# RMSNorm with repeated rows: ScalarE's table load moved ahead of gamma, and gamma issued in six pieces instead of seven

## The chip, the cores and the metric

The kernel runs on one core of one Trainium2 chip. The metric is the device time of one execution in microseconds. Executions of one kernel differ by some tenths of a microsecond, so every comparison below, unless it says otherwise, is between runs of the same rounds on the same chip.

## The reference

```python
x: (8, 512, 2048) float32, gamma: (2048,) float32
x_rep  = np.repeat(x, 2, axis=1)                       # every row twice
rms    = np.sqrt((x_rep ** 2).mean(axis=-1, keepdims=True) + 1e-6)
return (x_rep / rms * gamma[None, None, :])            # (8, 1024, 2048)
```

Each of the 4,096 rows is normalised once and written twice: 33.56 MB are read, 67.11 MB are written.

## The kernel before

The rows come in eight tiles of 128 partitions x 4 rows. A tile's buffer holds eight rows per partition; the load fills the last four, the scaled rows go to the even places and are copied to the odd ones, and one store of 8.39 MB takes all eight. There are three buffers, so three loads can go ahead of the first store, and the fourth needs the first store done.

```python
def load(i, eng, parts=1):                 # the first tile comes in two halves
    y = rows.tile([P, K * R, D], f32, name="y")
    step = K // parts
    for k in range(0, K, step):
        at = K * (R - 1) + k
        eng.dma_start(out=y[:, at : at + step, :], in_=x_t[i, :, k : k + step, :])
# ... cut: store (SyncE), square (ScalarE: Square with row sum, then Sqrt),
# ... scale (VectorE: reciprocal, then y * rstd * gamma), repeat (a copy)

def compute(i):
    for k in range(K):
        scale(i, k, square(i, k))
    repeat(i, 0, K // 2, nc.scalar.copy)
    repeat(i, K // 2, K, nc.vector.tensor_copy)

load(0, nc.sync, parts=2)
gamma_b = singles.tile([P, D], f32, name="gamma_b")
cuts = [0, *range(D // 4, D + 1, D // 8)]              # 512, then 6 x 256 values
for c0, c1 in zip(cuts, cuts[1:]):
    nc.scalar.dma_start(out=gamma_b[0:1, c0:c1], in_=gamma[c0:c1].partition_broadcast(1))
nc.gpsimd.partition_broadcast(out_ap=gamma_b[:], in_ap=gamma_b[0:1, :])
# ... cut: eps_t
load(1, nc.sync)
load(2, nc.sync)
loads_after = {2: (3, 4, 5), 4: (6, 7)}
for i in range(ntiles):
    compute(i)
    store(i, 0, K)
    for j in loads_after.get(i, ()):
        load(j, nc.sync)
```

The source names no semaphore. They are given to the transfers when the program is built: eight serve all loads, stores and gamma pieces, and a transfer that gets one again is held, in its issuing queue, until the transfer that had it has landed.

## Time and profile before

| | kernel before |
|---|---|
| median of 3 runs | 239.9 us (239.46 to 239.91) |
| profiled span | 237.9 us |
| gamma whole (the broadcast's wait ends) | 12.4 us |
| first scaling on VectorE | 14.92 us |
| first store issued | 27.05 us |
| first store landed | 52.8 us |

The times of single events are read from the timeline, the last one from the chain of waits. The lines themselves, and how to read them, stand in the prediction below.

### The profile page before, as it was taken

How to read it: one execution, taken by the hardware profiler on the slowest of the kernel's cores; microseconds unless marked ns; L12 is line 12 of the kernel's file. 1: busy time of each engine (PE TensorE's matmuls, PEld its weight loads, DVE VectorE, ACT ScalarE, POOL GpSimd, SP SyncE). 2: the span in 40 equal slices, each digit the busy share in tenths (PEclk: the TensorE clock that was granted, in tenths of full speed). 3: DMA queues.
4: the chain of work that ended last, by engine and by line, in shares of the span. 5: the costliest groups of instructions: out<-in, count | busy, mean ns of one | idle time of the engine just before them, and what ended most of it. 6: DMA issues, size and time to landing. Idle time of an engine off the chain costs nothing.

```text
span 237.9 us, 287 instructions
## 1 busy us (share of the span) xinstructions
DVE 96.5 (41%) x73; ACT 101.0 (42%) x106; POOL 2.5 (1%) x5
## 2 busy tenths in 40 slices
DVE  0049999960000000059999960000199990000000
ACT  2697999900000000099999920000599960000000
POOL 0030000000000000000000000000000000000000
DMA  7999998989899998999998999989998989999994
GB/s 265 436 446 441 441 441 353 530 353 496 386 452 430 397 485 353 441 441 441 441 518 364 464 419 430 452 369 430 435 518 364 518 364 485 397 452 430 408 474 176
DMA packets 2464, 100.69 MB, mean 423 GB/s; under 512 B 279, under 2 KB 285, under 8 KB 286
## 3 DMA queue, kind: packets, MB, share of 16 engines
q1 hardware_dynamic: 2448, 100.66, 98.5%
q14 instruction: 2, 0.02, 0.0%
q10 hardware_dynamic: 14, 0.01, 0.0%
HBM read 33.56 MB, written 67.11 MB: 423 GB/s over the span
## 4 chain that ended last, share of the span: by engine, by line
DMA 58%; ACT 12%; DVE 9%; issue 1%; POOLq 1%; ACTq 1%; SPq 0%
DMA y<-in_x_dram 33%; DMA out_dram<-y 21%; ACT sq L64 8%; DVE y L74 7%; DMA gamma_b<-in_gamma_dram 4%; ACT y L81 3%; DVE y L81 2%; ACT rms L68 1%; POOLq L136 1%; ACTq L95 1%; DVE rstd L73 0%; POOLq L96 0%; SPq L56 0%
## 5 line engine op out<-in xcount | busy, mean ns | idle before, releaser
L64 ACT ACTIVATE sq<-y 128x2048 f32<-128x2048 f32 x32 | 59.7, 1865 | 87.8 <-DMA y<-in_x_dram 87.8
L74 DVE SCALAR_TENSOR_TENSOR y<-y,rstd,gamma_b 128x2048 f32<-128x2048 f32 x32 | 75.3, 2352 | 4.1 <-POOL gamma_b L96 3.0
L73 DVE RECIPROCAL rstd<-rms 128x1 f32<-128x1 f32 x32 | 5.0, 158 | 94.6 <-ACT rms L68 94.3
L81 ACT COPY y<-y 128x4096 f32<-128x4096 f32 x8 | 28.7, 3590 | 1.4 <-DVE y L74 1.4
L81 DVE COPY y<-y 128x4096 f32<-128x4096 f32 x8 | 18.3, 2294 | 0.3
L68 ACT ACTIVATE rms<-ss,eps_t 128x1 f32<-128x1 f32 x32 | 9.4, 295 | 1.0
L64 ACT ACTIVATION_READ_ACCUMULATOR sq<-y 128x1 f32 x32 | 6.0, 187 | 0.0
L64 ACT ACT_TABLE_LOAD x1 | 1.3, 1283 | 3.0 <-issue 3.0
L96 POOL PARTITION_BROADCAST gamma_b<-gamma_b x1 | 2.3, 2294 | 12.2 <-DMA y<-in_x_dram 12.2
L68 ACT ACT_TABLE_LOAD x1 | 1.3, 1283 | 0.0
L98 DVE MEMSET eps_t<- 128x1 f32 x1 | 0.1, 59 | 0.8 <-PEq L125 0.8
L125 POOL MEMSET const-uint8-127<- 128x1 uint8 x1 | 0.1, 102 | 0.0
L125 POOL MEMSET const-bfloat16-1.0<- 128x1 bf16 x1 | 0.1, 101 | 0.0
L125 POOL MEMSET const-float32-0.0<- 128x1 f32 x1 | 0.1, 98 | 0.2 <-issue 0.2
L125 POOL MEMSET const-float32-1.0<- 128x1 f32 x1 | 0.1, 98 | 0.0
## 6 DMA issues: line engine op xcount, KB each, us to landing
y<-in_x_dram SPq DMA_DIRECT2D x7, 4096.0 KB, 14.6
y<-in_x_dram SPq DMA_DIRECT2D x2, 2048.0 KB, 7.4
out_dram<-y SPq DMA_DIRECT2D x8, 24.4
gamma_b<-in_gamma_dram ACTq DMA_DIRECT2D x6, 1.0 KB
gamma_b<-in_gamma_dram ACTq DMA_DIRECT2D x1, 2.0 KB
```

The costliest lines, as they stand in the source:

```text
L64: nc.scalar.activation(out=sq[:], in_=ys[i][:, K * (R - 1) + k, :], func=Act.Square, accum_out=ss[:])
L68: nc.scalar.activation(out=rms[:], in_=ss[:], func=Act.Sqrt, scale=inv_d, bias=eps_t[:])
L73: nc.vector.reciprocal(out=rstd[:], in_=rms[:])
L74: nc.vector.scalar_tensor_tensor(out=ys[i][:, R * k, :], in0=ys[i][:, K * (R - 1) + k, :], scalar=rstd[:], in1=gamma_b[:], op0=Alu.mult, o ...
L81: copy(out=y_r[:, k0:k1, 1, :], in_=y_r[:, k0:k1, 0, :])
L95: nc.scalar.dma_start(out=gamma_b[0:1, c0:c1], in_=gamma[c0:c1].partition_broadcast(1))
L96: nc.gpsimd.partition_broadcast(out_ap=gamma_b[:], in_ap=gamma_b[0:1, :])
L98: nc.vector.memset(eps_t, eps)
L125: nc = _bacc.Bacc("TRN2", target_bir_lowering=False, num_devices=1)
L136: with _tile.TileContext(nc) as tc:
```

## The change

It means to give ScalarE one table load in place of two and take it out of the first tile's work; and to take one transfer out of the start, so that the eight semaphores suffice and the first tile's second half need not wait for a gamma piece.

```diff
     load(0, nc.sync, parts=2)
+
+    nc.scalar.preload_act_table(Act.Sqrt)
     gamma_b = singles.tile([P, D], f32, name="gamma_b")
-    cuts = [0, *range(D // 4, D + 1, D // 8)]
+    cuts = [0, D // 4, *range(D // 2, D + 1, D // 8)]
```

## The prediction

> **What bounds the kernel now.** I read the page's transfer rows first, since the kernel reads 33.56 MB and writes 67.11 MB with little arithmetic.
>
> ```profile
> DVE 96.5 (41%) x73; ACT 101.0 (42%) x106; POOL 2.5 (1%) x5
> ...
> DMA packets 2464, 100.69 MB, mean 423 GB/s; under 512 B 279, under 2 KB 285, under 8 KB 286
> ...
> q1 hardware_dynamic: 2448, 100.66, 98.5%
> ```
>
> No compute engine works even half of the 237.9 us span, while the one queue that carries all loads and stores occupies its sixteen engines for 98.5% of it. To see where the other 1.5% lies I cut the span into stretches (columns: stretch, length, busy us of the three engines with counts, clock, share of the DMA engines, GB/s; packets count where they start, so a short stretch can pass 1.00):
>
> ```profile
> 0.00:2.00 2.00, 0.06 (x1) 0.00 (x0) 0.19 (x4) 1.00 0.45 91
> 2.00:4.00 2.00, 0.00 (x0) 1.02 (x1) 0.00 (x0) 1.00 0.77 295
> 4.00:8.00 4.00, 0.00 (x0) 0.26 (x1) 0.00 (x0) 1.00 0.97 414
> 8.00:12.00 4.00, 0.17 (x1) 3.85 (x5) 0.00 (x0) 1.00 1.02 439
> 12.00:16.00 4.00, 1.08 (x1) 3.94 (x6) 2.29 (x1) 1.00 1.07 463
> 16.00:27.00 11.00, 10.86 (x9) 9.56 (x9) 0.00 (x0) 1.00 1.02 441
> 27.00:33.00 6.00, 5.89 (x6) 5.90 (x10) 0.00 (x0) 1.00 1.19 448
> ...
> 60.00:120.00 60.00, 16.09 (x13) 18.63 (x21) 0.00 (x0) 1.00 1.01 435
> 120.00:180.00 60.00, 28.32 (x23) 28.77 (x32) 0.00 (x0) 1.00 0.98 425
> 180.00:232.00 52.00, 16.00 (x11) 14.08 (x14) 0.00 (x0) 1.00 1.01 440
> ```
>
> The DMA is full from 4 us to 232 us. Nothing drops where the computing starts (16 us), nor where the first store joins (27 to 33 us). So I treat the kernel as **transfers at full rate, plus an edge at each end**. From 33 us to 232 us the rows (with 430 GB/s in the 27 us not printed) average 432.6 GB/s; 100.69 MB at that rate is 232.8 us. In the first 4 us only 2 x 91 + 2 x 295 = 772 KB move instead of 1,730 KB: 2.2 us lost. 232.8 + 2.2 = 235.0; the other 2.9 us of the span are the last packets, the last landing and the closing barrier. The timed median, 239.9 us, is 2.0 us over the profiled span, which no change here touches.
>
> **A trap in the chain of waits.** In order of time it starts with gamma and the first tile's arithmetic:
>
> ```profile
> 2.69 9.71 DMA gamma_b<-in_gamma_dram
> ...
> 12.55 2.35 POOLq L136
> ...
> 14.92 2.35 DVE y L74
> ...
> 27.05 25.77 DMA out_dram<-y
> ```
>
> Read literally, gamma's arrival sets the end: an earlier gamma means an earlier first store. But that store's 25.77 us hold a queue. It is 8.39 MB (4,096 KB of loaded rows, doubled), which at 432.6 GB/s takes 19.4 us; the other 6.4 us it waited behind loads and for its first bytes. The three loads together are 12.58 MB, or 29.1 us at that rate; with the 2.2 us lost at the start they last till about 31.3 us. A first packet follows its issue by about 1 us (issue at 0.72 us, nothing moved before 1 us, 91 GB/s by 2 us). So the store, issued at 27.05 us, could have come till about 30.3 us: **3 us of slack**, an estimate from these rows.
>
> **What the Trainium skill says.** "ScalarE: Activation LUTs", section What ACT_TABLE_LOAD costs: about 1283 ns for a load, the same for every set, plus a drain of about 1380 ns at each switch. The trace has two loads of 1283 ns, so the first number agrees; the drain does not show, as the root begins at 11.43 us, 0.01 us after the load that began at 10.14. The page doesn't say in which sets Square lies; that one load serves Square and Sqrt is the change's claim. "DMA: Bandwidth & Descriptors", section Specifications, gives a fabric ceiling of 435 GB/s and an HBM limit of some 358 per core; the trace keeps 432.6, so here the first is the wall. The same page, section Queues, rings and completion order, says that each DMA engine takes turns between the queue rows that have work. Gamma's seven small pieces landing only by 12.4 us amid full-rate loads fits that.
>
> **The change, part by part.** The start of the timeline:
>
> ```profile
> 0.72 2.23 ACTq L95 DMA_DIRECT2D gamma_b<-in_gamma_dram  x7
> 0.72 8.20 SPq L52 DMA_DIRECT2D y<-in_x_dram  x4
> 2.98 1.28 ACT L64 ACT_TABLE_LOAD   x1 [2.98 <-issue]
> 10.14 1.28 ACT L68 ACT_TABLE_LOAD   x1
> 12.60 2.29 POOL L96 PARTITION_BROADCAST gamma_b<-gamma_b  x1 [12.17 <-DMA y<-in_x_dram]
> 14.92 2.35 DVE L74 SCALAR_TENSOR_TENSOR y<-y,rstd,gamma_b 128x2048 f32<-128x2048 f32 x1 [3.00 <-POOL gamma_b L96]
> ```
>
> *Table loads, two to one.* The first load now (2.98 us) lies in idle time: ScalarE waits for x until 8.12 us. The second is in ScalarE's work; without it the first root starts at about 10.15 instead of 11.43 us, 1.28 us sooner. But the first scaling waits from 11.92 to 14.92 us for the broadcast of gamma, not for the root. On the path: 0.
>
> *The load ahead of gamma.* ScalarE now issues gamma from 0.72 us; with 1.28 us of load first, from about 2.0 us. Cost to gamma: up to +1.28 us.
>
> *Six pieces, not seven.* One issue fewer is 0.27 us. More telling is how the pieces land: seven in 9.71 us after the last issue ended at 2.69. The first landed early, since the second load's 0.9 us wait for it (below) was over at about 2 us; the six others then shared about 8 us amid the packets of x, an estimated 1.2 to 1.3 us each. Afterwards all six pieces come into the busy period, and six did so before as well: the early one is the one saved. So gamma is whole at 12.4 us if the DMA engines set the pace, or at most 1.3 us later; I take +0.6. The broadcast, four scalings and a copy from gamma to the store took 27.05 - 12.42 = 14.63 us and stay, so the store is issued at 27.7 us (27.0 to 28.4), inside the slack. Cost at the end: 0.
>
> *The wait of the second half.* The queue's own waits:
>
> ```profile
> SPq L52 <- DMA y<-in_x_dram: 5.7, 1, 5.7
> SPq L52 <- DMA gamma_b<-in_gamma_dram: 0.9, 1, 0.9
> ```
>
> Nothing in the source makes x wait for gamma. Seven pieces and two halves are nine transfers; the eight semaphores that they use in the trace are then one too few, so the second half waited for the first piece. With six pieces there are eight, and the 0.9 us wait goes. It was worth nothing: the first half alone, 2.1 MB, keeps the engines busy for about 5 us, and the stretch from 4 to 8 us, in which one half hands over to the other, shows 0.97. The second tile's load keeps a wait for the eighth transfer before it, till about 8 us as now, with the first tile moving until about 12 us. On the path: 0.
>
> *Sum.* 0 + 0 + 0 + 0, with perhaps 0.1 us either way from who issues first at 0.72 us. Later stages keep their order and sizes.
>
> **Rivals.** *Gamma really is on the path*, as the chain says: then 0.6 to 1.3 us later gamma gives 240.5 to 241.2. The full windows from 16 to 33 us speak against it. *Gamma gets stuck behind the second half*, now issued at about 1.1 us, ahead of every piece: pieces that start only when the first tile has moved, at 12 us, need 6 x 1.26 = 7.6 us, so gamma is whole at about 19.6 us and the store goes at 34.2, some 4 us past the slack: 243.6 us, +1.6%. The taking of turns between queues speaks against it. *The second tile's load waits for the second half* (landing at about 12.5 us) and the DMA runs dry for 1 to 2 us: 241.5 us. Against it: of the eight transfers the first semaphore should go to the first half or to a gamma piece. *The start is the cost* and an earlier second half fills it: at most the 2.2 us of the first 4 us, 237.7 us; but the first half alone has packets enough there.
>
> **Range and chances.** All terms on the path are zero, so I predict the middle of the before-runs, slightly under the median: 239.7 us. The before-runs span 0.45 us; the bad rivals add 1 to 4 us at perhaps one in eight together, gains are at most tenths. Range 239.1 to 240.6. Two per cent is 4.8 us, more than any rival gives: faster 0.01, same 0.98, slower 0.01.
>
> **What would show it.** In the changed kernel's profile: one table load, at about 0.7 us, none before the first root; the second half issued at about 1.1 us with no wait for gamma; the broadcast starting between 12.5 and 14 us; the first store at 27.0 to 28.4 us, landing still at about 52.8 us; the DMA stretches from 4 to 232 us full as now; span 237.5 to 238.5 us. It is wrong if the DMA share dips near 12 us or between 28 and 36 us, or if the first store lands over 1 us later.

## The result, and the profile after

The changed kernel takes **239.67 us** (median of 6 runs, 239.34 to 239.86) against 239.91 us (6 runs, 239.4 to 240.17) of the kernel before. The ratio is 0.9993, with a 95% interval of 0.998 to 1.0007: the same. (The record calls a difference under 2% "the same"; here the interval holds 1 too. A ratio is the mean time of one kernel's fast runs over that of the other's of the same rounds, so it is not quite the ratio of the medians.)

The changed kernel's page shows what of the work has gone: ScalarE has 1.1 us and one instruction less. The queue of loads and stores is as full as it was.

```profile
DVE 96.5 (41%) x73; ACT 99.9 (42%) x105; POOL 2.5 (1%) x5
...
q1 hardware_dynamic: 2448, 100.66, 98.7%
```

The timeline of its start (start us, length us, engine, line, operation; in brackets the idle time before it and what ended that):

```profile
0.72 1.28 ACT L93 ACT_TABLE_LOAD   x1 [0.72 <-PEq L127]
0.72 8.28 SPq L52 DMA_DIRECT2D y<-in_x_dram  x4
0.75 1.93 ACTq L97 DMA_DIRECT2D gamma_b<-in_gamma_dram  x6
10.24 0.29 ACT L68 ACTIVATE rms<-ss,eps_t 128x1 f32<-128x1 f32 x1
11.41 2.29 POOL L98 PARTITION_BROADCAST gamma_b<-gamma_b  x1 [10.98 <-DMA gamma_b<-in_gamma_dram]
13.73 2.35 DVE L74 SCALAR_TENSOR_TENSOR y<-y,rstd,gamma_b 128x2048 f32<-128x2048 f32 x1 [3.01 <-POOL gamma_b L98]
25.86 0.35 SPq L56 DMA_DIRECT2D out_dram<-y  x1
```

Two things are to be seen. Gamma's first piece is issued at 0.75 us, **while** the table load runs from 0.72 to 2.00 us. And everything that hangs on gamma comes 1.19 us earlier than before: the broadcast (12.60 to 11.41 us), the first scaling (14.92 to 13.73 us), the first store (27.05 to 25.86 us).

Its chain of waits shows where those 1.19 us go (start us, us, what):

```profile
2.41 8.80 DMA gamma_b<-in_gamma_dram
...
25.86 26.76 DMA out_dram<-y
52.64 48.38 DMA y<-in_x_dram
```

The store that starts 1.19 us earlier takes 26.76 instead of 25.77 us to land, so that it lands at 52.62 instead of 52.82 us. Nearly all of the gain was spent in the queue behind the loads.

### The profile page after: what moved, and what is told of

Same layout as the page of the kernel before. It is cut to its first block, busy times and chain, and to the rows that moved or that the text cites. A ratio compares the mean times of both kernels' runs of the same rounds, so it can differ in the third digit from the quotient of the medians.

```text
span 237.6 us, 284 instructions
## 1 busy us (share of the span) xinstructions
DVE 96.5 (41%) x73; ACT 99.9 (42%) x105; POOL 2.5 (1%) x5
## 2 busy tenths in 40 slices
DMA packets 2462, 100.69 MB, mean 424 GB/s; under 512 B 278, under 2 KB 282, under 8 KB 284
## 4 chain that ended last, share of the span: by engine, by line
DMA 58%; ACT 12%; DVE 9%; issue 1%; POOLq 1%; ACTq 0%; SPq 0%
DMA y<-in_x_dram 33%; DMA out_dram<-y 21%; ACT sq L64 8%; DVE y L74 7%; DMA gamma_b<-in_gamma_dram 4%; ACT y L81 3%; DVE y L81 2%; ACT rms L68 1%; POOLq L138 1%; ACTq L97 0%; DVE rstd L73 0%; ACT L93 0%; POOLq L98 0%; SPq L56 0%
## 5 line engine op out<-in xcount | busy, mean ns | idle before, releaser
L93 ACT ACT_TABLE_LOAD x1 | 1.3, 1283 | 0.7 <-PEq L127 0.7
```

Source lines behind the costliest of these rows:

```text
L93: nc.scalar.preload_act_table(Act.Sqrt)
```

## The experiments

**The theory.** The time is set by 100.69 MB at the full rate of the sixteen transfer engines. The first store may be issued until the loads ahead of it run out; earlier than that is worth nothing, later counts in full. **The rival** is the chain of waits taken at its word: the first store is on the path, so each microsecond on gamma or the first tile's arithmetic moves the end by one. A second question is why gamma came earlier, where the prediction had it later.

### The first store, made late in steps

Three kernels are the changed one, with the first tile's last VectorE copy done two, four or six times more. The copies write the same data again, so the results stay right.

```diff
         repeat(i, K // 2, K, nc.vector.tensor_copy)
+        for _ in range(4 if i == 0 else 0):            # 2, 4 and 6
+            repeat(i, K // 2, K, nc.vector.tensor_copy)
```

> The changed kernel, with the last VectorE copy of the first tile done twice more (2.29 us each, same data), so that the first store goes 4.6 us later, at about 30.4 us. The loads' last packets start at about 32.4 us and a store's first packet follows its issue by about 1 us, so my theory has 1 us of slack left: 239.7 us, no change. If the first store is on the path, as the chain of waits says, +4.6 us: 244.3 us.

> Four more copies, 9.2 us: the store goes at about 35.0 us, past the slack (31.4 us) by 3.6 us. My theory: the transfer engines run dry near 33 to 36 us and the time is 239.7 + 3.6 = 243.3 us (range 242.5 to 244.5). If the first store is on the path: 248.9 us. If the transfers have spare room later on to make up for it: 239.7 us.

> Six more copies, 13.8 us: the store goes at about 39.6 us, 8.2 us past the slack. My theory: 239.7 + 8.2 = 247.9 us (range 247 to 249), 4.6 us more than with four copies, since past the slack each microsecond counts in full. If the first store is on the path: 253.5 us. If there is room to make up: less than 4.6 us between this run and the one with four copies.

| copies added | first store issued | median | over the kernel before of the same rounds (239.4 us) | ratio, 95% interval |
|---|---|---|---|---|
| 2 | 30.31 us | 240.07 us (4 runs) | 0.67 us | 1.0017 (0.999 to 1.0043) |
| 4 | 34.97 us | 244.74 us (4 runs) | 5.34 us | 1.0217 (1.0195 to 1.024) |
| 6 | 39.74 us | 249.52 us (4 runs) | 10.12 us | 1.0417 (1.0395 to 1.0439) |

The issue times stand in the SyncE timelines, one line of each of the three runs:

```profile
30.31 24.67 SPq L56 DMA_DIRECT2D out_dram<-y  x3
34.97 24.67 SPq L56 DMA_DIRECT2D out_dram<-y  x3
39.74 24.67 SPq L56 DMA_DIRECT2D out_dram<-y  x3
```

From four to six copies the issue moves by 4.77 us and the time by 4.78 us: past the slack each microsecond counts in full. Going back at that slope to the time of the kernel before gives a break-even at 34.97 - 5.34 = 29.63 us, and 39.74 - 10.12 = 29.62 us from the other run. So, with these copies in, the first store may be issued until about **29.6 us**, give or take half a microsecond by the intervals; the run with two copies, 0.7 us past it, is within the noise. By this the kernel before had 29.6 - 27.05 = 2.6 us of slack and the changed kernel has 3.8 us. The rival, which wanted 244.3, 248.9 and 253.5 us, is out.

My own expectations were off, by about 1.4 us with four copies and 1.6 us with six, outside both ranges. A small part is where the transfers run dry. I had taken 32.4 us in the changed kernel for the start of the loads' last packets. The trace shows the loads' completion marks and the first store's packets starting there; the loads' last data packets start by 31.0 us and take 2.0 us each, which fits the first store's packets already sharing the engines with them. Where the store is late they take 1.2 us and the loads are through sooner: with four copies the trace shows no data packet at work between 31.8 and 35.8 us, 4.0 us where I had expected 3.6. The stretches (columns as in the prediction) show the same hole, first of the changed kernel, then with six copies:

```profile
32.00:36.00 4.00, 3.93 (x4) 4.00 (x2) 0.00 (x0) 1.00 1.21 524
36.00:40.00 4.00, 3.96 (x3) 3.94 (x7) 0.00 (x0) 1.00 0.94 410
```

```profile
32.00:36.00 4.00, 3.93 (x3) 0.00 (x0) 0.00 (x0) 1.00 0.00 0
36.00:40.00 4.00, 3.93 (x4) 0.00 (x0) 0.00 (x0) 1.00 0.00 0
```

VectorE is as busy in one as in the other. The DMA columns tell them apart: nothing moves for 8 us.

The larger part of the miss is not lost at the first store at all. The landings, from the completion marks in the traces (us, in brackets the difference from the kernel before):

| | kernel before | 2 copies | 4 copies | 6 copies |
|---|---|---|---|---|
| first store | 52.82 | 51.66 (-1.16) | 55.79 (+2.97) | 60.57 (+7.75) |
| fourth tile's load | 101.15 | 100.55 (-0.60) | 105.23 (+4.08) | 109.99 (+8.84) |
| fourth store | 140.22 | 140.89 (+0.67) | 145.30 (+5.08) | 150.37 (+10.15) |

Between the first and the fourth store each of the three loses another 1.8 to 2.4 us. The copies hold back the later tiles too (the second store is issued at 47.15 us with four copies, at 39.22 us in the kernel before), but what costs these 2 us was not tested. So 29.6 us is a break-even of the whole program with the copies in it. The hole alone says something later: the store's first packet followed its issue by 0.8 us (34.97 to 35.81 us) and the engines ran dry at 31.8 us, so a store issued by about 31.0 us, an estimate from these, leaves no hole.

### The transfers alone

```diff
-        for k in range(K):
-            scale(i, k, square(i, k))
-        repeat(i, 0, K // 2, nc.scalar.copy)
-        repeat(i, K // 2, K, nc.vector.tensor_copy)
+        nc.vector.tensor_copy(out=ys[i][:, 0:K, :], in_=ys[i][:, K : 2 * K, :])
```

> Wrong result on purpose: the arithmetic of each tile is replaced by one VectorE copy of the four loaded rows, so all loads and stores stay as they are and every store can go earlier. If the transfers alone set the time, 239.0 to 240.0 us, though the first store goes at about 18 to 19 us, 7 us or more earlier. If computing at the start or in later stages is on the path, faster by the part that it holds: 7 us for the first store alone (233 us).

Measured: 239.24 us (5 runs), against 239.5 us (9 runs) of the kernel before; ratio 0.999, interval 0.9977 to 1.0002. The result is wrong, as intended. Its SyncE timeline has the first store 9.2 us earlier than in the kernel before:

```profile
17.84 20.36 SPq L56 DMA_DIRECT2D out_dram<-y  x3
```

With all the arithmetic gone but one copy a tile, and every store free to go sooner, at most 0.23% is won, and perhaps nothing. That bounds what any change to the table loads, gamma or the arithmetic could have earned here.

### Gamma in one piece

```diff
-    cuts = [0, D // 4, *range(D // 2, D + 1, D // 8)]
+    cuts = [0, D]
```

> Gamma in one transfer. My theory of the turns: the first piece gets in before the packets of x (landed at about 2.1 us), each later one waits its turn, so one piece is whole by about 2.2 us, the broadcast is over before x has arrived (8.2 us), the first scaling starts at about 10.7 us, the third waits for the second half at about 13 us, and the first store goes at about 24 us, 3 us earlier than before. Time: if the transfers set the end, 239.7 us, within 0.3% of before. If the first store is on the path, as the chain of waits says, 236.9 us (1.3% faster).

Measured: 240.33 us (5 runs) against 239.5 us; ratio 1.0021 (1.0007 to 1.0035). Gamma was whole at 2.93 us, later than the 2.2 us expected; the first scaling came as expected and the first store about 1 us earlier:

```profile
3.02 2.29 POOL L98 PARTITION_BROADCAST gamma_b<-gamma_b  x1 [2.59 <-DMA gamma_b<-in_gamma_dram]
...
10.76 2.35 DVE L74 SCALAR_TENSOR_TENSOR y<-y,rstd,gamma_b 128x2048 f32<-128x2048 f32 x1
```

The broadcast now starts 9.6 us earlier than before and the first store is issued at 22.89 us, 4.16 us earlier. The end does not come earlier. The kernel is 0.2% slower, if anything; I did not pursue a difference of that size, and its cause stays open.

### Which part brought gamma forward, and what the table load does

The first of these kernels has the six pieces but no preloaded table, the second the preload but the seven old pieces.

```diff
-    nc.scalar.preload_act_table(Act.Sqrt)              # six_only: the changed kernel without this
-    cuts = [0, D // 4, *range(D // 2, D + 1, D // 8)]  # preload_only: the changed kernel with
+    cuts = [0, *range(D // 4, D + 1, D // 8)]          #   the old cuts
```

> Six pieces, both table loads where they were. If the dropped piece alone explains gamma's earlier arrival (about 1.2 us a piece), gamma is whole at 11.2 us, the broadcast starts at 11.4 and the first scaling at about 13.7 us, although the root waits for its table load until 11.43 us; first store at 25.9 us; no queue wait for gamma. If the preload had a share in it, the first scaling is later than 13.9 us. Time within 0.3% of before.

Measured: 239.97 us (4 runs) against 239.5 us; ratio 1.0017 (1.0003 to 1.003), within the 0.3% expected.

```profile
11.11 2.29 POOL L96 PARTITION_BROADCAST gamma_b<-gamma_b  x1 [10.69 <-DMA gamma_b<-in_gamma_dram]
...
13.44 2.35 DVE L74 SCALAR_TENSOR_TENSOR y<-y,rstd,gamma_b 128x2048 f32<-128x2048 f32 x1 [1.49 <-POOL gamma_b L96]
```

The first store is issued at 25.57 us. So the dropped piece alone brings gamma forward. The preload has no share: the root waited for its table until 11.46 us and was still in time for gamma. One expectation failed: a queue wait for gamma is left.

```profile
SPq L52 <- DMA gamma_b<-in_gamma_dram: 0.6, 1, 0.6
```

The second half goes at 1.16 us and does not wait. The wait is that of the second tile's load, which in this trace shares the semaphore of gamma's first piece and goes at 2.21 us, instead of 8.11 us in the kernel before. So dropping a piece does not by itself end the sharing, and issuing the second tile's load 5.9 us earlier is worth nothing either.

> The table load ahead of gamma, with the seven old pieces. If the load does not hold up the issue of transfers behind it (as the trace of the changed kernel suggests: first piece issued at 0.75 us, while the load runs to 2.00 us), gamma is whole at 12.3 to 12.5 us as in the kernel before, the second half waits for the first piece again (about 0.9 us), the first store goes at about 27.0 us. If the load delays the issues, as my prediction took it, gamma is whole at 13.2 us or later and the store goes at about 28.3 us. Time in both cases within 0.3% of the kernel before, as the store has slack; if gamma is on the path that sets the end, 239.9 us and no gain at all against before.

Measured: **242.39 us** (4 runs) against 239.5 us; ratio 1.0118 (1.0104 to 1.0131), under 2% but clear of the noise. Neither side of the expectation had this. Gamma's first piece is issued at 0.74 us, so the load does not hold up the issues. But gamma was whole at 8.64 us, earlier than either theory said, and the kernel is 2.9 us slower. The queue's waits, the SyncE timeline and the stretches of this kernel:

```profile
SPq L52 <- DMA y<-in_x_dram: 7.0, 1, 7.0
```

```profile
8.09 1.28 SPq L52 DMA_DIRECT2D y<-in_x_dram  x3
```

```profile
4.00:8.00 4.00, 0.00 (x0) 0.00 (x0) 0.00 (x0) 1.00 0.78 333
8.00:12.00 4.00, 1.00 (x2) 3.87 (x4) 2.29 (x1) 1.00 0.77 258
```

Three loads are issued from 8.09 us on: the second half and the two whole tiles. In the kernel before, the second half had gone at 2.03 us. In the trace it now waits on, and then uses, the same semaphore as the first half (with the table load ahead of gamma, the first half takes the first of the eight, which gamma's first piece had before), so it waited 7.0 us until the first half had landed; between 7.7 and 9.1 us no packet of x was at work. From 4 to 12 us, 4 x (333 + 258) = 2,364 KB moved, against 4 x (414 + 439) = 3,412 KB before. The missing 1,048 KB are 2.4 us at the kernel's 432.6 GB/s, most of the 2.9 us. Gamma was early for the same reason: in the trace its last four pieces met no packets of x on their engine and started between 7.41 and 7.55 us.

The next kernel tests whether the order of the semaphores is the cause, and not the preload as such. The seven pieces stay, and the table load moves behind the first of them:

```diff
-    nc.scalar.preload_act_table(Act.Sqrt)
     for c0, c1 in zip(cuts, cuts[1:]):
         nc.scalar.dma_start(out=gamma_b[0:1, c0:c1], in_=gamma[c0:c1].partition_broadcast(1))
+        if c0 == 0:
+            nc.scalar.preload_act_table(Act.Sqrt)
```

> Seven pieces and the table load as in the run with the preload alone, but the load stands behind the first piece instead of ahead of it. That run was 1.2% slower: its second half waited on the first half's own semaphore, was issued at 8.09 us, and the transfers ran dry near 8 us. If the cause is which transfer shares a semaphore with the second half, and the table load itself costs nothing, the first piece takes the first semaphore again, the second half waits for it until about 2 us as in the kernel before, gamma is whole at about 12.4 us, and the time is 239.7 us. If a preloaded table with seven pieces is slow for a reason of its own, 242.4 us again.

Measured: 239.68 us (4 runs) against 239.49 us (11 runs); ratio 1.0005 (0.9993 to 1.0018). The queue's waits of this kernel:

```profile
SPq L52 <- DMA y<-in_x_dram: 5.7, 1, 5.7
...
SPq L52 <- DMA gamma_b<-in_gamma_dram: 0.9, 1, 0.9
```

The second half waits for gamma's first piece again, not for x, and is issued at 2.01 us; the 2.9 us are gone. The cost was the semaphore that the second half got. This kernel also isolates the wait that the change removed: it has the one table load, seven pieces and the 0.9 us wait, and its ratio to the kernel before, 1.0005, is as near to 1 as the changed kernel's 0.9993 in its own rounds.

### An attempt to beat both

```diff
+            if i == 0 and k == 0:        # the first half's two rows from two queues
+                nc.sync.dma_start(out=y[:, at : at + 1, :], in_=x_t[i, :, 0:1, :])
+                nc.scalar.dma_start(out=y[:, at + 1 : at + 2, :], in_=x_t[i, :, 1:2, :])
+                continue
# and cuts = [0, D]
```

> An attempt to beat both: one of the first tile's first two rows per partition is issued from ScalarE and the other from SyncE, and gamma is one piece behind it. The start loses 2.2 us of transfers in the first 4 us, of which about 1.7 us pass before any packet; at best the slow first packets overlap and 0.3 to 0.8 us are won (239.0 us). If the first packets are slow for a cause that two queues share, 239.7 us, the same.

Measured: 239.82 us (6 runs) against 239.49 us; ratio 1.0014 (1.0 to 1.0027). The first 4 us move 2 x 49 + 2 x 291 = 680 KB, not more than the 772 KB before. The start is not gained by a second queue. No version with a right result beats either kernel.

## Why the prediction was right

- **The bound and the sum.** Predicted 239.7 us (239.1 to 240.6) and "same"; measured 239.67 us and ratio 0.9993. The step that carried it, transfers at full rate plus two edges, is confirmed from both sides: without the arithmetic the kernel is not measurably faster, and with the first store past its slack it slows one for one.
- **The trap in the chain, and the slack.** Predicted 3 us of slack, with a break-even at about 30.3 us. The late stores put the break-even at 29.6 us by the time of the whole program, and at about 31.0 us by the hole alone: 2.6 to 4 us of slack, with the prediction in between. The first store landed 0.2 us earlier for an issue 1.19 us earlier, as "landing still at about 52.8 us" said.
- **Two table loads to one.** Predicted 1.28 us sooner for the first root and 0 on the path. The root came at 10.24 instead of 11.43 us, and the scaling still waited 3.01 us for the broadcast.
- **The load ahead of gamma: wrong.** The step said "with 1.28 us of load first, from about 2.0 us". The first piece was issued at 0.75 us, during the load.
- **Six pieces: wrong as a consequence.** The step said that "the early one is the one saved", and took +0.6 us for gamma. Since the issues were not delayed, the first piece still got in early: by the trace it landed at 2.08 us (2.01 us before), and the others at 6.73, 8.00, 8.66, 9.93 and 11.21 us, each within 0.1 us of the same piece before. The piece saved was the last one, which had landed at 12.40 us. So the first store was issued at 25.86 us and not within 27.0 to 28.4 us. The error was 1.84 us and cost nothing, because an early store is worth nothing. That was luck in part: as far to the other side, at about 29.5 us, it would have used up the slack of the kernel with the copies. (A smaller slip: the chain's line says that the last issue began at 2.69 us, not that it ended then; it ended at 2.95 us.)
- **The wait of the second half.** Predicted as gone, with the second half issued at about 1.1 us, and worth 0. It was issued at 1.16 us and no wait for gamma is left. The wait's worth of 0 is shown by the kernel with the load behind the first piece.
- **What the sum did not see.** I worked the parts out one by one, each as 0. The runs show that they are not independent: the preload with seven pieces costs 1.2%. Going from seven pieces to six is what makes this preload harmless, as it leaves a free semaphore for the second half. The prediction had counted that free semaphore, but only as the end of a 0.9 us wait worth nothing. The third rival, the transfers running dry on a wait for the wrong transfer, was the right kind of danger, but at the second half and not at the second tile.

## What to carry to other kernels

When a transfer stands in the chain of waits, work out how long its own bytes take. If it took much longer than that from issue to landing, it may have queued, and an earlier issue may be worth nothing; make it late in known steps to measure how much slack it had. Count the transfers in flight against the semaphores there are, and look which earlier transfer each one shares with: moving an instruction that touches no transfer at all made one load wait 7.0 us for another and cost 1.2%.

## What the Trainium skill lacked or had wrong

- "ScalarE: Activation LUTs", section What ACT_TABLE_LOAD costs, gives the load's duration, and 1283 ns held in every trace that I read. It does not say that transfers queued on the same engine behind the load are issued while it runs: issue at 0.75 us in a load from 0.72 to 2.00 us.
- The same section adds a drain of about 1380 ns to each switch. The kernel before shows none: its root begins at 11.43 us, 0.01 us after the end of the load.
- The same page, section Table sets, does not say where Square lies. One load, made for Sqrt, served Square, Sqrt and the copies in all kernels here that preload it and do the arithmetic, with right results.
- "DMA: Bandwidth & Descriptors", section Specifications, gives some 0.6 us to the first byte for transfers issued from SyncE or ScalarE. It does not say from when it counts. Here the first packet of x starts at 1.74 us in the changed kernel for an issue that began at 0.72 us and took 0.38 us: about 1.0 us from its start, 0.6 us from its end.
- The same section's limit of some 358 GB/s of HBM per core did not bind for this one core: 432.6 GB/s from 33 to 232 us in the kernel before. The row does not say that it is meant for both cores of a pair at work; the page's section Bandwidth does. No run here has a second core.
- The same page, section Queues, rings and completion order, describes turns of a whole packet, typically of several descriptors. Here the later gamma pieces mostly landed 1.27 us apart, about the time of two of the 16 KB transfers that the profile lists one by one (0.61 us each). One small piece, or its completion, for each of them would fit, but that is inferred. The second piece of the kernel before, issued at 1.26 us, began only at 5.65 us, so longer turns stood before.
